# The plain tiles of a SwiGLU layer as a chunk of their own: chunks of 3, 7, 6 and 6 tiles in place of 4, 6, 6 and 6

## The chip, the cores and the metric

The kernel runs on one core of one Trainium2 chip. The core has a matrix engine (TensorE, PE in the profile, whose weight loads are PEld), a vector engine (VectorE, DVE), a scalar engine (ScalarE, ACT), a general engine (GpSimd, POOL) and SyncE (SP), which here only issues DMA transfers. Each engine works off its own instructions in order and waits for the others through semaphores. The metric is the device time of one execution in microseconds.

## The reference

A hybrid decoder trunk of two layers over 528 tokens (16 meta tokens and 512 others), with 1024 channels, in float32. Each layer has two half-step feed-forward blocks around a token mixer; every block is normalized ahead and behind:

```python
def swiglu(x, w_in, w_out):
    gate, up = jnp.split(x @ w_in, 2, axis=-1)
    return (jax.nn.silu(gate) * up) @ w_out

h = h + 0.5 * rmsnorm(swiglu(rmsnorm(h, g[0]), w_ffn_in[layer, 0], w_ffn_out[layer, 0]), g[1])
```

The gate and the up projection have 2816 columns each. That is 22 tiles of 128 hidden channels, each of which needs one block of gate and one of up weights (1024 x 128 each) and later one 128-row slice of `w_out`. There are four such feed-forward blocks, called l0f0, l0f1, l1f0 and l1f1 here; the tensor names of the profile leave out the last digit (`hidl1f` belongs to l1f0 and l1f1). The mixers between them, gated linear attention in layer 0 and windowed attention in layer 1, are not touched by the change. In the second layer the blocks run over the 512 tokens behind the meta tokens alone, in products of 256 or 512 columns; in the first over all 528, in products of 264, or of 272 and 256.

## The kernel before

**Three products for one.** Float32 precision is reached on the fast matmul type by splitting both operands into a high and a low part (`fp32r`). `mm3s` issues for each 128 x 128 block high times high, low times high and high times low. Every weight therefore passes through ACT (copy to the high part, L231 or L251) and DVE (subtraction to the low part, L232 or L252) before PE can use it.

**Weights.** `load_unit` issues the DMAs of a weight unit from SP into raw tiles of 128 x 512 (a pool of `RAWS` = 11), `split_unit` and `split_pair` split them into pair tiles of a second pool (`SLOTS` = 32). `set_ahead(n, slots)` says how far the loads may run ahead and how many slots the split weights may hold at once; a split that finds no slot waits until a product that used one has been issued (`slot`, `free_slots`).

**A feed-forward block** (`ffn`) takes its 22 tiles in the chunks of `FF_CHUNKS`. For each chunk the hidden tiles (named `hid...`) are made first, and then their part of the output projection (`out_proj`, `out_steps`; the products are named `y`) is added to the sum `Y` (named `Y`): the first chunk's part is written by ACT (L608), the later ones are added by DVE (L610).

- The first `PLAIN` = 3 tiles are made plainly: `x_first` makes the first two tiles (four units of 1024 x 128 weights) while the layer's input is still being normalized, and `x_units` makes the third tile. Their products are named `x`. Behind each stands a chain over DVE (L663, scale), ACT (L664, silu), DVE (L667, gate times up), ACT (L426, high part of hidden) and DVE (L427, low part).
- All other tiles are made by a Strassen scheme (class `Strassen`): gate and up are two rows, the two halves of the channels are the inner index, the two halves of the tokens are the columns, and seven block products replace eight. Each product is 4 x 3 = 12 matmuls. The products are called `11`, `s1`, `s2`, `12`, `s3`, `s4`, `22` after the weight part on the left; they go to PSUM tiles `a`, `c`, `d` (and `e` in a chunk's last tile). A zero matmul (`d<-zeros`) opens each chunk's tile `d`. The product `11` of the next tile stands ahead of `s4` and `22` of the tile at hand.
- The right sides of four of the products are sums of blocks of the layer's input. `right_factors` makes them once per block: eight scaled copies on ACT (L743, `xs...`), ten sums on DVE (L739), and eight splits (`z..._t`, four sums of two pieces: ACT L729 for the high part, DVE L730 for the low part). The weight sums `s1` to `s4` are made by accumulating DMAs from POOL (L257) and sums on DVE (L267, L272).

In the kernel before, the first chunk has three plain tiles and one Strassen tile, so its products that take a `z` stand right behind the third plain tile.

**Order.** The program is written by a small scheduler (`Flow`, `Job`), which runs in Python while the kernel is built: generators stand for chains of work, each `yield` gives an estimated delay, and the matmuls advance a modelled clock (`mm`). What a chain issues is placed in the program when the modelled clock reaches it. The order on every engine is thus fixed before the kernel runs. A waiting instruction holds up all those behind it on its engine.

In `out_steps`, when `jobs` are given, products of the first output rows with all hidden tiles but the last are placed ahead of the wait for the last one (`begin`).

Of the kernel before, what the change touches and what calls it, by code (L numbers as in the profile page):

```python
# [20 lines left out]
SEQ = 512  # L21
TOK = META + SEQ
NFF = 22
FF_CHUNKS = [(0, 4), (4, 10), (10, 16), (16, 22)]
LAST = 16
PLAIN = 3
NLAST = NFF - LAST
# [4 lines left out]
L1W = [(16, 512)]  # L32
SLOTS = 32
RAWS = 11
RING = 8
STEP = 1.1
LANDED = 2.2
ADDED = 2.5
# [90 lines left out]
def trunk_kernel(ctx: ExitStack, tc, a, out):  # L129
    nc = tc.nc  # L130
    pe, act, dve, pool, sp = nc.tensor, nc.scalar, nc.vector, nc.gpsimd, nc.sync
    flow = Flow()
# [19 lines left out]
    def pair_tile(name, dt=F32R):  # L152
        return hp.tile([P, 2, TOK], dt, tag="pair", name=name)

    def duo(name):
        t = pair_tile(name, F32)
        return t[:, 0], t[:, 1]
# [4 lines left out]
    def gain(layer, i, k):  # L162
        c = V_GAIN + layer * 48 + i * 8 + k
        return vec[:, c : c + 1]
# [19 lines left out]
    for layer in range(2):  # L184
        for f in range(2):
            for lo, hi in FF_CHUNKS:
                for t in range(lo, hi):
# [26 lines left out]
    def set_ahead(n, slots=None):  # L214
        ahead[0], limit[0] = n, slots or n
        room[0].finish(flow)
        room[0] = Job(None)
# [206 lines left out]
    def split(dst, src, g):  # L424
        o, n = g
        act.activation(dst[:, 0, o : o + n], src, AF.Copy)  # L426
        dve.tensor_tensor(dst[:, 1, o : o + n], src, dst[:, 0, o : o + n].bitcast(F32), op=ALU.subtract)  # L427
# [148 lines left out]
    def out_proj(*args, **named):  # L576
        for _ in out_steps(*args, **named):
            pass
# [71 lines left out]
    def ffn(x, groups, finish, opening=False, tail=4):  # L650
        set_ahead(8 if opening else 16)

        def evac_to(hids):
            gss = {}

            def evac(i, g, p):
                o, n = g
                r = x.rt[:, o : o + n]
                if i % 2 == 0:
                    if i not in gss:  # L660
                        gss[i] = duo("gu")
                    gs = gss[i][0][:, o : o + n]
                    dve.tensor_tensor(gs, p[:, :n], r, op=ALU.mult)  # L663
                    act.activation(gs, gs, AF.Silu)  # L664
                else:
                    gs, us = (t[:, o : o + n] for t in gss[i - 1])
                    dve.tensor_tensor(us, p[:, :n], gs, op=ALU.mult)  # L667
                    split(hids[i // 2], us, g)

            return evac  # L670

        jobs = []
        n2 = sum(n for _, n in groups) // 2
        halves = [(groups[0][0], n2), (groups[0][0] + n2, n2)]
        z = {}
        finish.x = x

        def new_hid():
            hids.append(pair_tile(f"hid{x.name}_{lo + len(hids)}"))
            return hids[-1]  # L680

        for ci, (lo, hi) in enumerate(FF_CHUNKS):
            hids = []
            if ci == 0:
                jobs = x_first(x, 4, evac_to([new_hid() for _ in range(2)]), opening)
                set_ahead(16, 4)
                flow.spawn(right_factors(x, halves, z))
                for t in range(2, PLAIN):
                    jobs += x_units(x, 2, groups, evac_to([new_hid()]))
                set_ahead(16, 8)  # L690
            else:
                set_ahead(16, RING)
            tiles = Strassen(x, z, halves)
            cur = tiles.head(new_hid())
            while cur:
                tiles.body(cur)
                nxt = tiles.head(new_hid()) if len(hids) < hi - lo else None
                if nxt is None:
                    fin = (finish, KD, True) if lo >= LAST else (None, 0, False)
                    if ci == 0:  # L700
                        flow.wait(*jobs)
                    proj = out_steps(hids, groups, x.groups, ci == 0, *fin, jobs)
                    end = used[0] + NLAST + tail
                jobs.append(tiles.tail(cur, proj if nxt is None else None))
                cur = nxt
            if lo >= LAST:
                set_ahead(32)
                cap[0] = min(end, len(units))
            for _ in proj:
                pass  # L710
# [538 lines left out]
    x = Operand("l0f0", lambda k: gain(0, 0, k), L0)  # L1249
# [48 lines left out]
    def into(name, layer, i, half, gv, groups, ffn=True):  # L1298
        nxt = Operand(name, gv, groups, ffn)
        return nxt, Residual(name, layer, i, half, nxt)  # L1300


    nxt, fin = into("l0m", 0, 1, True, lambda k: gain(0, 2, k), L0, False)
    ffn(x, L0, fin, True)
    x = nxt
    nxt, fin = into("l0f1", 0, 3, False, lambda k: gain(0, 4, k), L0)
    gla(x, fin)
    x = nxt
    nxt, fin = into("kv", 0, 5, True, lambda k: vec[:, V_KVN + k : V_KVN + k + 1], L0)
    ffn(x, L0, fin, tail=8)  # L1310


    with tc.tile_pool(name="kp", bufs=1) as kp:
        x = Operand("l1f0", lambda k: gain(1, 0, k), L1)
# [8 lines left out]
        nxt, fin = into("l1m", 1, 1, True, lambda k: gain(1, 2, k), L1, False)  # L1323
        ffn(x, L1W, fin)
        x = nxt
        nxt, fin = into("l1f1", 1, 3, False, lambda k: gain(1, 4, k), L1)
# [87 lines left out]
```

## Time and profile before

| | us |
|---|---|
| three runs | 1943.03, 1938.41, 1940.04 |
| median | 1940.04 |
| profiled execution, its own time | 1938.74 |
| span of the profiled execution, first to last instruction | 1937.0 |
| PE busy within the span | 1880.3 (97%) |
| DVE busy | 1377.9 (71%) |
| ACT busy | 1048.9 (54%) |
| POOL busy | 323.2 (17%) |
| mean granted clock of PE | 0.99 of full |

The profile is of one execution. A row of the timeline gives start, duration, engine, line, operation, out<-in and how many instructions are drawn together, then in brackets the idle time ahead of it and who ended it. Durations of neighbouring matmuls overlap (a matmul's end is modelled), so what a run of matmuls takes is read from start to start. A row of the windows view gives for one stretch its length, the busy time of PE, PEld, DVE, ACT and POOL with counts, the clock granted to PE (1.00 is full), and the DMA share and rate.

### The profile page before, as it was taken

To read this page: it belongs to the slowest core of one execution; us is meant where nothing else is said; L and a number is where in the kernel's file an instruction comes from. 1 tells how busy PE (TensorE), PEld (TensorE's weight loads), DVE (VectorE), ACT (ScalarE), POOL (GpSimd) and SP (SyncE) were. 2 spreads that over 40 slices of the span, in tenths; PEclk is the share of its full clock that TensorE was granted. 3 is DMA by queue.
4 is the path that set the end of the run, shared out by engine and by line. 5 is a ranking of instruction groups with operands and counts; after the bars stand their busy time and mean duration, and the time that the engine had idled before them with its cause. 6 is when DMAs were issued, how large, how long until landed. Compare 5 with 4: busy or idle time off the path is not lost.

```text
span 1937.0 us, 37708 instructions
## 1 busy us (share of the span) xinstructions
PE 1880.3 (97%) x14374; PEld 1789.6 (92%) x14374; DVE 1377.9 (71%) x2745; ACT 1048.9 (54%) x2349; POOL 323.2 (17%) x449
## 2 busy tenths in 40 slices
PE   8999999999999999999999999999988998999997
PEld 8999999999999999999999898989966897989897
DVE  7685858775464858585887685858798676858585
ACT  8563636663246755363675553636655675536363
POOL 2101010311212210101032101010342131010102
PEclk9999999999999999999999999999999998999998
DMA  6656565322113165656650556565320305565651
GB/s 200 152 141 154 141 153 157 97 80 74 38 62 110 49 153 137 153 143 152 161 150 24 142 139 160 143 160 164 101 77 23 88 23 143 140 159 143 166 144 44
DMA packets 134982, 234.44 MB, mean 121 GB/s; under 512 B 15120, under 2 KB 27920, under 8 KB 134800
## 3 DMA queue, kind: packets, MB, share of 16 engines
q1 hardware_dynamic: 112624, 192.04, 31.0%
q0 software_dynamic: 21888, 39.86, 13.6%
q8 instruction: 112, 1.84, 0.4%
q14 instruction: 70, 0.57, 0.1%
q10 hardware_dynamic: 288, 0.13, 0.0%
HBM read 229.87 MB, written 2.10 MB: 120 GB/s over the span
## 4 chain that ended last, share of the span: by engine, by line
PE 76%; DVE 13%; ACT 6%; issue 3%; DMA 1%; POOL 0%; SPq 0%; DVEq 0%; ACTq 0%; POOLq 0%
PE y L167 28%; PE a L167 18%; PE x L167 11%; PE c L167 8%; PE d L167 5%; DVE w L232 1%; PE e L167 1%; PE o L167 1%; ACT w L231 1%; DVE H L488 1%; DVE w L252 1%; DVE w_s L252 1%; PE po L167 1%; ACT w_s L251 1%; DMA raw<-in_w_last 0%
## 5 line engine op out<-in xcount | busy, mean ns | idle before, releaser
L252 DVE TENSOR_TENSOR w_s<-raw,w_s 128x512 fp32r<-128x512 f32 x304 | 207.8, 688 | 142.1 <-ACT w_s L251 140.7
L257 POOL DMA_DIRECT2D raw<-in_w_in x152 | 133.4, 929 | 1032.3 <-DMA raw<-in_w_in 363.0
L167 PE MATMUL y<-hidl0f,w 128*128 128x256 f32 (+1 forms) x2112 | 261.4, 285 | 0.0
L232 DVE TENSOR_TENSOR w<-raw,w 128x512 fp32r<-128x512 f32 x362 | 234.4, 667 | 35.9 <-ACT w L231 33.1
L167 PEld LDWEIGHTS y<-hidl0f,w 128*128 128x128 f32 x2112 | 259.1, 188 | 0.2
L251 ACT ACTIVATE w_s<-raw 128x512 fp32r<-128x512 f32 x304 | 184.7, 626 | 130.0 <-DVE raw L267 75.9
L167 PE MATMUL y<-hidl1f,w 128*128 128x512 f32 (+1 forms) x1344 | 250.2, 346 | 0.0
L167 PEld LDWEIGHTS y<-hidl1f,w 128*128 128x128 f32 x1344 | 211.9, 188 | 32.4
L231 ACT ACTIVATE w<-raw 128x512 fp32r<-128x512 f32 x362 | 198.8, 584 | 54.4 <-PE y L167 44.9
L252 DVE TENSOR_TENSOR w<-raw,w 128x512 fp32r<-128x512 f32 x228 | 153.4, 687 | 41.0 <-ACT w L251 38.4
L251 ACT ACTIVATE w<-raw 128x512 fp32r<-128x512 f32 x228 | 137.4, 620 | 43.7 <-PE y L167 42.6
L167 PE MATMUL x<-x_l0m,w 128*128 128x272 f32 (+1 forms) x1200 | 157.6, 288 | 0.0
L167 PEld LDWEIGHTS x<-x_l0m,w 128*128 128x128 f32 x1200 | 149.2, 189 | 1.1
L610 DVE TENSOR_TENSOR Y<-y,Y 128x256 f32<-128x256 f32 (+2 forms) x176 | 82.2, 472 | 68.6 <-PE y L167 68.2
L167 PE MATMUL a<-zl0f_t,w_s 128*128 128x264 f32 x912 | 125.1, 286 | 3.0 <-ACT w_s L251 1.7
L167 PE MATMUL a<-zl1f_t,w_s 128*128 128x256 f32 x912 | 121.5, 282 | 0.1
L167 PEld LDWEIGHTS a<-zl0f_t,w_s 128*128 128x128 f32 x912 | 116.5, 188 | 4.7 <-ACT w_s L251 1.9
L167 PEld LDWEIGHTS a<-zl1f_t,w_s 128*128 128x128 f32 x912 | 113.1, 188 | 2.0 <-ACT c L797 1.5
L422 POOL TENSOR_TENSOR acc_post<-acc_post,sq_post 128x256 f32<-128x256 f32 (+1 forms) x72 | 62.2, 864 | 252.4 <-ACT sq_post L421 251.3
L814 ACT ACTIVATE c<-c 128x264 f32<-128x264 f32 (+1 forms) x76 | 32.0, 421 | 131.4 <-DVE c L813 131.4
L167 PE MATMUL x<-x_l0f,w 128*128 128x272 f32 (+1 forms) x576 | 75.5, 292 | 6.7 <-ACT w L231 5.7
L167 PEld LDWEIGHTS x<-x_l0f,w 128*128 128x128 f32 x576 | 73.5, 193 | 7.8 <-ACT w L231 5.7
(368 smaller groups left out, 3533.4 us busy)
## 6 DMA issues: line engine op xcount, KB each, us to landing
raw<-in_w_in SPq DMA_DIRECT2D x428, 256.0 KB, 3.6
raw<-in_w_in POOLq DMA_DIRECT2D x152, 256.0 KB, 5.1
raw<-in_w_out SPq DMA_DIRECT2D x96, 256.0 KB, 3.4
raw<-in_gla_in SPq DMA_DIRECT2D x50, 256.0 KB, 3.3
raw<-in_w_last SPq DMA_DIRECT2D x48, 256.0 KB, 2.9
raw<-in_w_out SPq DMA_DIRECT2D x64, 128.0 KB, 2.9
raw<-in_gla_out SPq DMA_DIRECT2D x16, 256.0 KB, 2.7
raw<-in_w_q SPq DMA_DIRECT2D x16, 256.0 KB, 4.2
```

The costliest lines, as they stand in the source:

```text
L167: inst = pe.matmul(o, lhs, rhs, start=start, stop=stop, skip_group_check=onto)
L231: act.activation(w[:, 0, :m], raw[:, :m], AF.Copy)
L232: dve.tensor_tensor(w[:, 1, :m], raw[:, :m], w[:, 0, :m].bitcast(F32), op=ALU.subtract)
L251: act.activation(w[:, 0, :512], src, AF.Copy)
L252: dve.tensor_tensor(w[:, 1, :512], src, w[:, 0, :512].bitcast(F32), op=ALU.subtract)
L257: pool.dma_start(dst, src, accum_op=ALU.add)
L422: pool.tensor_tensor(sums[0][:, :n], sums[0][:, :n], t[:, :n], op=ALU.add)
L488: dve.tensor_tensor(h, t, h, op=ALU.add)
L610: dve.tensor_tensor(y, p[:, :n], y, op=ALU.add)
L814: act.activation(t.u2, t.u2, AF.Silu)
```

## The change

`FF_CHUNKS` becomes 3, 7, 6 and 6 tiles. The first chunk now holds the three plain tiles alone. When their hidden tiles are issued, the output projection of these three follows at once, and the loop goes on to the next chunk; no product is placed ahead of the wait for the third hidden tile by `begin`, since no `jobs` are given to `out_steps` there. The job that makes the sums of operand blocks (`right_factors`) is kept in `factors`, and the second chunk's first Strassen tile is issued after it. Seven tiles are in the second chunk, of which each is made as before.

The slot limit follows: 4 slots while the sums are being made (as before), 8 once they are issued (`widen`), and in the Strassen chunks `RING` less the chunk's tiles: 14 - 7 = 7 slots in the second chunk, 14 - 6 = 8 in the third and fourth, where it was 8 in all.

The units of `w_out` change their width: a unit of the first chunk has 8 row blocks of 3 x 128 = 384 columns (before 512), a unit of the second 7 x 128 = 896 columns, loaded as 512 and 384 (before 512 and 256).

```diff
-FF_CHUNKS = [(0, 4), (4, 10), (10, 16), (16, 22)]
+FF_CHUNKS = [(0, 3), (3, 10), (10, 16), (16, 22)]
...
-RING = 8
+RING = 14
...
                 jobs = x_first(x, 4, evac_to([new_hid() for _ in range(2)]), opening)
                 set_ahead(16, 4)
-                flow.spawn(right_factors(x, halves, z))
+                factors = flow.spawn(right_factors(x, halves, z))
+
+                def widen():
+                    yield factors
+                    set_ahead(16, 8)
+
+                flow.spawn(widen())
                 for t in range(2, PLAIN):
                     jobs += x_units(x, 2, groups, evac_to([new_hid()]))
-                set_ahead(16, 8)
-            else:
-                set_ahead(16, RING)
+                flow.wait(*jobs)
+                out_proj(hids, groups, x.groups, True)
+                continue
+            flow.wait(factors)
+            set_ahead(16, RING - (hi - lo))
             tiles = Strassen(x, z, halves)
...
-                    if ci == 0:
-                        flow.wait(*jobs)
-                    proj = out_steps(hids, groups, x.groups, ci == 0, *fin, jobs)
+                    proj = out_steps(hids, groups, x.groups, False, *fin, jobs)
```

Lines below the edit stand six further down in the changed kernel: L729, L730, L739 and L743 are L735, L736, L745 and L749 there.

The instructions of all engines are the same in number and kind, but for the widths told above and four zero matmuls less (one for each first chunk). Their order differs only in the first two chunks of each of the four blocks.

TensorE in l1f1, behind the last `x` product of the third plain tile. In the kernel before, the order is this (`w_11`, `w_s` and `w_12` are weight parts, `zl1f_t` a sum of operand blocks; what a row waits for stands in brackets):

```order
L167 MATMUL x_0_19459<-x_l1f_7_19109,w_1_19337 128x512 x3
L167 MATMUL d_19505<-zeros 128x256
L167 MATMUL a_0_19501<-x_l1f_0_18931,w_11_19469 128x256 [waits PE_49,Activation_49]
L167 MATMUL a_0_19501<-x_l1f_0_18931,w_11_19469 128x256 [waits DVE_49]
...
L167 MATMUL c_0_19503<-zl1f_t_19537,w_s_19486 128x256 [waits PE_49,Activation_49]
L167 MATMUL c_0_19503<-zl1f_t_19537,w_s_19486 128x256 [waits DVE_49]
L167 MATMUL d_19505<-x_l1f_4_19034,w_12_19540 128x256 [waits Activation_49]
```

In the changed kernel the same place has the output projection of the three plain tiles (`y_0_16` and `y_1_16` are the first and second output rows, `hidl1f_0` to `hidl1f_2` the three hidden tiles):

```order
L167 MATMUL x_0_19439<-x_l1f_7_19085,w_1_19321 128x512 x3
L167 MATMUL y_0_16_19481<-hidl1f_0_19025,w_0_19324 128x512 [waits Activation_49]
L167 MATMUL y_0_16_19481<-hidl1f_0_19025,w_0_19324 128x512 [waits DVE_49] x2
L167 MATMUL y_0_16_19481<-hidl1f_1_19026,w_0_19324 128x512 [waits Activation_49]
L167 MATMUL y_0_16_19481<-hidl1f_1_19026,w_0_19324 128x512
L167 MATMUL y_0_16_19481<-hidl1f_1_19026,w_0_19324 128x512 [waits DVE_49]
L167 MATMUL y_1_16_19494<-hidl1f_0_19025,w_0_19327 128x512 [waits PE_49]
L167 MATMUL y_1_16_19494<-hidl1f_0_19025,w_0_19327 128x512
L167 MATMUL y_0_16_19481<-hidl1f_2_19386,w_0_19324 128x512 [waits Activation_49]
```

The products with `zl1f_t` have moved behind the 72 matmuls of the output projection, and the third hidden tile is now asked for by the ninth matmul behind the last `x` product.

VectorE at the same place, between the low parts of the second and the third hidden tile. Before:

```order
L427 TENSOR_TENSOR hidl1f_1_19050<-gu,hidl1f_1_19050 128x256 [waits Activation_49]
L252 TENSOR_TENSOR w_11_19469<-raw_0_19382,w_11_19469 128x512 [waits DMAHW6_49,Activation_49]
L739 TENSOR_TENSOR xsl1f_0_19407<-xsl1f_4_19409,xsl1f_0_19407 128x2x256 [waits Activation_49]
L739 TENSOR_TENSOR xsl1f_4_19409<-xsl1f_4_19409,xsl1f_0_19407 128x2x256 [waits DVE_49]
L252 TENSOR_TENSOR w_s_19486<-raw_3_19385,w_s_19486 128x512 [waits DMASW2_49,Activation_49]
L667 TENSOR_TENSOR gu<-x_0_19459,gu 128x512 [waits PE_49]
L739 TENSOR_TENSOR xsl1f_2_19408<-xsl1f_6_19410,xsl1f_2_19408 128x2x256 [waits Activation_49]
L739 TENSOR_TENSOR xsl1f_4_19409<-xsl1f_4_19409 128x2x256 [waits DVE_49]
L427 TENSOR_TENSOR hidl1f_2_19402<-gu,hidl1f_2_19402 128x512 [waits Activation_49]
```

In the changed kernel:

```order
L427 TENSOR_TENSOR hidl1f_1_19026<-gu,hidl1f_1_19026 128x256 [waits Activation_49]
L745 TENSOR_TENSOR xsl1f_0_19391<-xsl1f_4_19393,xsl1f_0_19391 128x2x256 [waits Activation_49]
L667 TENSOR_TENSOR gu<-x_0_19439,gu 128x512 [waits PE_49]
L745 TENSOR_TENSOR xsl1f_2_19392<-xsl1f_6_19394,xsl1f_2_19392 128x2x256 [waits Activation_49]
L745 TENSOR_TENSOR xsl1f_4_19393<-xsl1f_4_19393,xsl1f_0_19391 128x2x256 [waits DVE_49]
L427 TENSOR_TENSOR hidl1f_2_19386<-gu,hidl1f_2_19386 128x512 [waits Activation_49]
L232 TENSOR_TENSOR w_0_19498<-raw_0_19378,w_0_19498 128x384 [waits DMAHW2_49,Activation_49]
```

The two splits of the first Strassen tile's weights and one of the sums have moved behind the third hidden tile's last instruction.

ScalarE in l1f1, ahead of the second half of the plain tiles' evacuation. Before, two splits of a plain unit stand there (L231), followed by three scaled copies (L743). In the changed kernel four splits of `w_out` units have come in between:

```order
L231 ACTIVATE w_1_19321<-raw_512_19203 128x512 [waits DMAHW5_49]
L231 ACTIVATE w_0_19324<-raw_0_19205 128x384 [waits DMAHW6_49]
L231 ACTIVATE w_0_19327<-raw_0_19207 128x384 [waits DMAHW7_49]
L231 ACTIVATE w_0_19342<-raw_0_19209 128x384 [waits DMAHW0_49]
L231 ACTIVATE w_0_19345<-raw_0_19211 128x384 [waits DMAHW1_49]
L749 ACTIVATE xsl1f_0_19391<-H,vec 128x512 x2
L399 ACT_TABLE_LOAD
L399 ACTIVATE R_l1f_19102<-st_l1f_272_19372,eps 128x256 [waits PE_49]
```

One scaled copy that stood ahead of the table load now stands behind it, and the four splits stand ahead of it.

## The prediction, made before the changed kernel was run

> **What bounds the kernel now.** I read the page first, then the chain of work that ended last, then PE's waits, and last the four places that the change touches.
>
> ```profile
> span 1937.0 us, 37708 instructions
> PE 1880.3 (97%) x14374; PEld 1789.6 (92%) x14374; DVE 1377.9 (71%) x2745; ACT 1048.9 (54%) x2349; POOL 323.2 (17%) x449
> PE 76%; DVE 13%; ACT 6%; issue 3%; DMA 1%; POOL 0%; SPq 0%; DVEq 0%; ACTq 0%; POOLq 0%
> ```
>
> PE is busy for 97% of the span, and three quarters of the chain are its own. The amount of PE's work hardly changes here, so the change can only win what PE idles, or works at a lower clock. What PE waited for, longest first (total, times, longest one); these four rows fall into the first chunks:
>
> ```profile
> PE c L167 <- ACT zl1f_t L729: 11.1, 2, 6.4
> ...
> PE d L167 <- ACT w L251: 1.8, 1, 1.8
> PE a L167 <- ACT w_s L251: 1.7, 1, 1.7
> ...
> PE c L167 <- ACT zl0f_t L729: 1.6, 1, 1.6
> ```
>
> The largest wait in the program is for the sums of operand blocks (`zl1f_t`) in layer 1. The timeline of PE at its worst place, l1f1, shows how it stands:
>
> ```profile
> 1596.86 0.28 PE L167 MATMUL d<-zeros 128*128 128x256 f32 x1
> 1597.85 0.38 PE L167 MATMUL a<-x_l1f,w 128*128 128x256 f32 x1 [0.72 <-ACT w L251]
> 1598.58 1.55 PE L167 MATMUL a<-x_l1f,w 128*128 128x256 f32 x11 [0.34 <-DVE w L252]
> 1606.51 0.80 PE L167 MATMUL c<-zl1f_t,w_s 128*128 128x256 f32 x2 [6.38 <-ACT zl1f_t L729]
> ...
> 1610.16 2.27 PE L167 MATMUL d<-x_l1f,w 128*128 128x256 f32 x11
> 1612.26 1.11 PE L167 MATMUL e<-x_l1f,w_s 128*128 128x256 f32 x8
> ```
>
> The plain tiles' products end at 1596.86. Three Strassen products (`a`, `c`, `d`) then take until 1612.26. Eleven matmuls of `d` needed 2.10 us there (1610.16 to 1612.26), much more than elsewhere, so idle time is not all. The windows view from the last plain product to the end of the third Strassen product, for l0f0, l0f1, l1f0, l1f1 (length, then busy time of PE, PEld, DVE, ACT and POOL with counts; the third number from the end is the granted clock):
>
> ```profile
> 47.00:54.40 7.40, 4.95 (x39) 4.54 (x38) 7.16 (x14) 6.67 (x14) 0.00 (x0) 1.00 0.31 94
> 672.40:683.40 11.00, 6.75 (x38) 5.82 (x37) 10.07 (x18) 6.93 (x15) 0.94 (x2) 0.85 0.42 131
> 1068.20:1079.70 11.50, 6.74 (x38) 6.52 (x37) 9.63 (x16) 7.10 (x14) 0.88 (x1) 0.70 0.35 81
> 1597.00:1612.20 15.20, 7.51 (x38) 6.66 (x37) 13.42 (x23) 10.27 (x20) 0.87 (x1) 0.66 0.38 97
> sum 45.10, PE 25.95 PEld 23.53 DVE 40.28 ACT 30.97 POOL 2.70; mean PE 6.49 PEld 5.88 DVE 10.07 ACT 7.74 POOL 0.67
> ```
>
> So 45.10 us for 12 products. DVE is nearly full there (40.28 of 45.10): it makes the sums, and PE waits for it through ACT. In three of the four the clock fell too (0.85, 0.70, 0.66). What undisturbed work takes is read from start to start:
>
> ```profile
> 122.31 1.63 PE L167 MATMUL a<-x_l0f,w 128*128 128x264 f32 x12
> ...
> 125.23 1.64 PE L167 MATMUL a<-zl0f_t,w 128*128 128x264 f32 x12
> ...
> 132.55 1.61 PE L167 MATMUL a<-x_l0f,w 128*128 128x264 f32 x12
> 147.81 33.42 PE L167 MATMUL y<-hidl0f,w 128*128 128x256 f32 x273
> 181.07 0.29 PE L167 MATMUL d<-zeros 128*128 128x264 f32 x1
> 1703.97 30.19 PE L167 MATMUL y<-hidl1f,w 128*128 128x512 f32 x129
> 1733.99 0.28 PE L167 MATMUL d<-zeros 128*128 128x256 f32 x1
> 1734.11 1.57 PE L167 MATMUL a<-x_l1f,w 128*128 128x256 f32 x12
> ```
>
> Seven products between 122.31 and 132.55: 1.463 us each at 264 columns, by proportion 1.42 at 256. A `y` matmul takes 33.26 / 273 = 0.122 us in layer 0 and 30.02 / 129 = 0.233 us (512 columns) in layer 1. Twelve products should take 6 x 1.463 + 6 x 1.42 = 17.3 us. The loss is 45.1 - 17.3 = **27.8 us**: 3.0, 6.6, 7.2 and 10.9 in the four blocks.
>
> **The change, part by part.**
>
> *The Strassen tile leaves the first chunk.* It moves to the second chunk with its 84 matmuls, its evacuation, its weights and its part of the output projection; none of it is saved. Gone is the wait: -27.8, if the sums are done when the second chunk begins, and if the place is not taken by another wait.
>
> *Four zero matmuls less.* 1733.99 to 1734.11 is 0.12 us; four are -0.5.
>
> *The sums beside the output projection.* PE now has 72 `y` matmuls of 0.233 us, 16.8 us, in each block of layer 1, and 144 of 0.122, 17.6 us, in layer 0. In that time DVE has 20 instructions to issue between the third hidden tile and the second chunk (eight splits of `z`, three sums, four splits of `w_out`, four of weight parts, one sum of weight parts); at 0.6 us each, as the DVE rows below follow each other, that is 12 us. In l1f1 it starts at about 1602 and PE ends its `y` at 1597.3 + 1.6 + 16.8 = 1615.7 (worked out below), so 1.7 us are left. The last sums are not needed at the first product either but up to seven products later. Cost 0; if that cover is gone, a `z` comes late again in the second chunk (a rival).
>
> *What is late next: the third hidden tile.* Before, the Strassen products stood between the third plain tile and the output projection. Now the ninth matmul behind the last plain product asks for it. In l1f1 its chain was (ACT rows, then DVE rows):
>
> ```profile
> 1586.22 0.42 ACT L426 ACTIVATE hidl1f<-gu 128x256 fp32r<-128x256 f32 x1 [1.01 <-DVE gu L667]
> 1586.55 1.14 ACT L231 ACTIVATE w<-raw 128x512 fp32r<-128x512 f32 x2
> 1587.59 1.94 ACT L743 ACTIVATE xsl1f<-H,vec 128x512 f32<-128x512 f32 x3
> ...
> 1601.10 0.63 ACT L426 ACTIVATE hidl1f<-gu 128x512 fp32r<-128x512 f32 x1 [0.94 <-DVE gu L667]
> ```
>
> ```profile
> 1596.40 0.76 DVE L427 TENSOR_TENSOR hidl1f<-gu,hidl1f 128x256 fp32r<-128x256 f32 x2 [0.38 <-ACT hidl1f L426]
> ...
> 1600.39 0.68 DVE L667 TENSOR_TENSOR gu<-x,gu 128x512 f32<-128x512 f32 x1
> ...
> 1602.19 0.68 DVE L427 TENSOR_TENSOR hidl1f<-gu,hidl1f 128x512 fp32r<-128x512 f32 x1
> ```
>
> Two things shift it. Four `w_out` splits of 384 columns now stand ahead of ACT's table load: between 0.33 us (256 columns, 1586.22 to 1586.55) and 0.52 (512 columns, 1586.55 to 1587.59 for two), so about 0.42 each, 1.7 in all; one scaled copy of 0.65 went behind. The queue is 1.0 us later, and so are the first two hidden tiles: PE waits some 0.5 us at its first `y`. Against that, DVE has two weight splits and a sum less between L427 and L667, 1.9 us. Step by step: ACT ends the second hidden tile at about 1597.65, two copies at 1598.95, DVE the sum at 1599.6 and L667 at 1600.2, ACT the high part at 1600.85. PE, started at 1597.3, has run its eight matmuls by 1599.2 and waits 1.6. In l1f1 that is **+2.1** (bounds 0.5, the first wait alone, and 4.0: nothing won on DVE, so that the high part comes 1.0 behind its 1601.73 of before, 3.5 behind 1599.2).
>
> In l0f1 the rows are these:
>
> ```profile
> 673.99 0.43 ACT L426 ACTIVATE hidl0f<-gu 128x272 fp32r<-128x272 f32 x1 [1.91 <-DVE gu L667]
> ```
>
> ```profile
> 673.51 0.77 DVE L667 TENSOR_TENSOR gu<-x,gu 128x272 f32<-128x272 f32 x2
> ```
>
> The plain products end at 672.3, nine `y` matmuls at 0.122 cover 1.1 us, until 673.4. The high part was there at 674.4. The queue's shift (+1.0 to +1.7) and two weight splits fewer on DVE (-1.2) leave it between 674.1 and 676.0: a wait of 0.7 to 2.6. I take **+1.4**, nearer the lower end, since DVE and not ACT released L426 here. In l0f0 and l1f0 L667 waited for PE itself, so the queues have room and the splits of `w_out` fit into it:
>
> ```profile
> 46.83 0.77 DVE L667 TENSOR_TENSOR gu<-x,gu 128x272 f32<-128x272 f32 x2 [0.31 <-PE x L167]
> ```
>
> ```profile
> 1068.30 0.69 DVE L667 TENSOR_TENSOR gu<-x,gu 128x512 f32<-128x512 f32 x1 [0.27 <-PE x L167]
> ```
>
> The high part then comes about 1.3 us behind the last plain product, and eight or nine `y` matmuls cover 1.1 to 1.9. I take **+0.1** each (0 to 1.4, the latter what l0f1 is given).
>
> *The clock.* The rows above show it at 1.00 in l0f0, with 7.40 us that held 3.0 of loss, and at 0.85 in l0f1, where 0.15 x 11.0 = 1.65 us were lost to it. A wait as I expect it in l0f1 or l1f1 lies between these; I charge one such drop, **+1.65** (bounds 0 and four of them, 6.6). [...]
>
> *Seven slots instead of eight in the second chunk.* The slot goes to the seventh hidden tile. DVE's split of the next tile's part `11` is the last of the two in this row:
>
> ```profile
> 129.89 1.29 DVE L252 TENSOR_TENSOR w<-raw,w 128x512 fp32r<-128x512 f32 x2
> ```
>
> It starts at 130.5 and is used at 132.55. With seven slots it needs the slot of product `22` of the tile before, issued at 125.23 and done by 126.7, with nearly 4 us to spare (ACT's half needs some 0.6 of them). Cost 0 (bounds 0 and one product per tile, the rival below).
>
> *Narrower `w_out` units.* DMAs to landing:
>
> ```profile
> raw<-in_w_out SPq DMA_DIRECT2D x96, 256.0 KB, 3.4
> ...
> raw<-in_w_out SPq DMA_DIRECT2D x64, 128.0 KB, 2.9
> ```
>
> 192 KB lie between. They are issued in the order of use, no wait of PE's above names a DMA, and their number is the same: 0.
>
> The sum: -27.8 - 0.5 + 0.1 + 0.1 + 1.4 + 2.1 + 1.65 = -22.95. The profiled execution took 1938.74 us (span 1937.0), so the changed kernel would take 1915.8 by it. The median shown is 1.3 above the profiled one; I forecast for the median **1917 us**, a gain of 23.
>
> **The rivals.**
>
> *The third hidden tile becomes the new stall.* ACT and DVE are in-order queues, and the sums stand among the instructions that make it. If all four blocks wait 2.1 us and drop the clock once each, that is 4 x (2.1 + 1.65) = 15.0 in place of 5.35: 1917 + 9.65 = 1927. For it speaks that DVE is nearly full in these stretches; against it, that two of the blocks have room in the queues, and that fewer instructions stand ahead of it than before.
>
> *Seven slots choke the second chunk (slower).* If every part came one product later and none of it were covered, each of the tiles would lose a product: 7 x (2 x 1.463 + 2 x 1.42) = 40 us, 1957. It decides from 23 / 28 = 0.82 us per tile of the second chunk. The lead of part `11` is only 1.4 us (131.2 to 132.55), which speaks for it; the slot that is free 4 us ahead speaks against.
>
> *The sums are late all the same.* If DVE gets behind during the output projection, the second chunk starts with the old wait. With some 2 us to spare and 12 us to do, a fifth more of DVE time would use that up; 2 us per block would give 1917 + 8 = 1925.
>
> **How the numbers follow.** Forecast 0.68, hidden tile 0.17, slots 0.08, sums late 0.07. A difference under 0.2% (3.9 us) can't be told from no change here. Faster by more: the forecast, the hidden tile and half of the last case, whose price can grow past 2 us per block: 0.88. Slower: the slots, 0.08. Within: the other half of the last case, 0.04. The forecast's own range is 1911 to 1924: all new waits at their lower ends and no drop gives -27.8 - 0.5 + 1.2 = -27.1, 1913, less 2 for the spread of the runs; the upper bounds of the two waits and two more drops give some 7 more. With the second and the fourth case the range is 1909 to 1931.
>
> **What would show it.** Right: no row of PE waiting for `zl1f_t` or `zl0f_t` above 1 us; PE going from `x` to `y` at 47, 672, 1068 and 1597 (less the gain so far), with short waits there for L426 and L427; a granted clock near 1.00 in these stretches but for one; the second chunk's products at 1.42 to 1.46 us from start to start. Wrong: waits of PE for L251 or L252 at the parts of the second chunk (slots), or a wait for `z` at its start (sums late), or waits for `hidl0f` and `hidl1f` of over 3 us (hidden tile).

## The result and the profile after

| | before | changed |
|---|---|---|
| runs, us | 1943.03, 1938.41, 1940.04, 1941.07 | 1920.44, 1918.89, 1919.28, 1919.39 |
| median, us | 1940.55 | 1919.34 |
| profiled execution, us | 1938.74 | 1920.44 |
| its span, us | 1937.0 | 1918.7 |

The ratio is 0.9891, with a 95% interval of 0.9874 to 0.9908: 21.2 us less at the medians, where 23 were forecast. The head of the page and the chain of the changed kernel:

```profile
span 1918.7 us, 37680 instructions
PE 1877.7 (98%) x14370; PEld 1786.4 (93%) x14370; DVE 1379.7 (72%) x2741; ACT 1045.8 (55%) x2349; POOL 322.9 (17%) x449
PE 72%; DVE 15%; ACT 6%; DMA 4%; issue 3%; POOL 0%; SPq 0%; DVEq 0%; ACTq 0%; POOLq 0%
```

But for four zero matmuls on PE and four additions on VectorE (2741 instructions for 2745), all engines do the same work as before. The additions are those that each chunk's last Strassen tile needs for its product in `e`; the account of the change above names the zero matmuls alone. PE's waits (total, times, longest):

```profile
PE y L167 <- ACT hidl1f L426: 1.8, 2, 1.4
...
PE y L167 <- ACT hidl0f L426: 1.5, 1, 1.5
...
PE a L167 <- ACT c L803: 0.8, 2, 0.5
```

The rows for `zl1f_t` and `zl0f_t` are gone; the waits for the third hidden tile have come. Where they lie, on PE's timeline in l0f1 and in l1f1:

```profile
668.83 1.27 PE L167 MATMUL y<-hidl0f,w 128*128 128x272 f32 x9
671.65 16.65 PE L167 MATMUL y<-hidl0f,w 128*128 128x272 f32 x135 [1.55 <-ACT hidl0f L426]
688.14 0.29 PE L167 MATMUL d<-zeros 128*128 128x264 f32 x1
688.26 1.62 PE L167 MATMUL a<-x_l0f,w 128*128 128x264 f32 x12
689.72 1.64 PE L167 MATMUL c<-zl0f_t,w_s 128*128 128x264 f32 x12
```

```profile
1587.48 2.12 PE L167 MATMUL y<-hidl1f,w 128*128 128x512 f32 x8 [0.40 <-ACT hidl1f L426]
1591.00 15.08 PE L167 MATMUL y<-hidl1f,w 128*128 128x512 f32 x64 [1.40 <-ACT hidl1f L426]
1605.91 0.28 PE L167 MATMUL d<-zeros 128*128 128x256 f32 x1
1606.03 1.58 PE L167 MATMUL a<-x_l1f,w 128*128 128x256 f32 x12
1607.44 1.59 PE L167 MATMUL c<-zl1f_t,w_s 128*128 128x256 f32 x12
```

The products of the second chunk follow each other at 1.41 to 1.46 us with no idle time before a `z`. The windows view of the four output projections of plain tiles (length, busy PE, PEld, DVE, ACT, POOL; the third number from the end is the granted clock):

```profile
47.04:64.61 17.57, 17.57 (x147) 17.57 (x146) 14.52 (x25) 14.90 (x36) 3.48 (x4) 1.00 0.65 177
668.83:688.14 19.31, 17.76 (x146) 17.55 (x145) 16.58 (x28) 15.08 (x36) 2.57 (x3) 1.00 0.49 121
1059.73:1076.53 16.80, 16.80 (x74) 13.37 (x73) 13.64 (x23) 13.93 (x27) 2.60 (x3) 1.00 0.53 132
1587.08:1605.91 18.83, 17.03 (x72) 13.40 (x73) 17.39 (x31) 16.44 (x33) 2.75 (x4) 1.00 0.59 137
```

The clock is at 1.00 in all four. DVE and ACT are now nearly full in the output projection (17.39 and 16.44 of 18.83 us in l1f1), where PE is too.

To see what each block won, I take the time from the end of its plain products to the begin of its third chunk. Both kernels do the same work between these marks: seven Strassen tiles and the output projection of ten tiles. The marks are read from PE's timelines; the forecast column repeats the terms of the prediction by block (loss, less new waits, plus a zero matmul).

| | before, us | changed, us | won | forecast |
|---|---|---|---|---|
| l0f0 | 134.1 | 130.3 | 3.8 | 3.0 |
| l0f1 | 137.2 | 132.1 | 5.1 | 5.3 |
| l1f0 | 133.3 | 126.6 | 6.7 | 7.3 |
| l1f1 | 137.1 | 128.5 | 8.6 | 9.0 |
| sum | 541.7 | 517.6 | 24.1 | 24.6, less 1.65 for a clock drop |

These marks repeat well: a second profile of the changed kernel gives 517.7. The spans, however, differ by 18.3 only. Of the other 5.8, 5.0 were lost where nothing was changed: from l1f0's fourth chunk to the end of l1f1's plain products, mostly the attention mixer of layer 1, the profile of before took 301.9 us and that of after 306.9. The windows view of 100 us of that mixer, of before and of the changed kernel:

```profile
1415.01:1515.01 100.00, 88.53 (x608) 61.29 (x607) 85.84 (x241) 54.70 (x228) 26.75 (x26) 0.97 0.15 46
```

```profile
1400.18:1500.18 100.00, 88.48 (x586) 60.68 (x584) 83.01 (x232) 52.98 (x221) 26.78 (x26) 0.91 0.14 46
```

PE has the same order of work there and was busy as long, but 22 matmuls less got done at a clock of 0.91 in place of 0.97. By these rounded figures 9 of the 100 us went to the lower clock there in place of 3, which is the size of the whole difference. How far this is chance is taken up with the repeated runs below.

### The profile page after: what moved, and what is told of

Same layout as the page of the kernel before. It is cut to its first block, busy times and chain, and to the rows that moved or that the text cites. A ratio compares the mean times of both kernels' runs of the same rounds, so it can differ in the third digit from the quotient of the medians.

```text
span 1918.7 us, 37680 instructions
## 1 busy us (share of the span) xinstructions
PE 1877.7 (98%) x14370; PEld 1786.4 (93%) x14370; DVE 1379.7 (72%) x2741; ACT 1045.8 (55%) x2349; POOL 322.9 (17%) x449
## 4 chain that ended last, share of the span: by engine, by line
PE 72%; DVE 15%; ACT 6%; DMA 4%; issue 3%; POOL 0%; SPq 0%; DVEq 0%; ACTq 0%; POOLq 0%
PE y L167 29%; PE a L167 16%; PE x L167 11%; PE c L167 7%; PE d L167 4%; DMA raw<-in_w_in 2%; DVE w L252 1%; DVE w L232 1%; PE o L167 1%; PE e L167 1%; DVE H L488 1%; DVE w_s L252 1%; ACT w L231 1%; DMA raw<-in_w_last 1%; PE po L167 1%
## 5 line engine op out<-in xcount | busy, mean ns | idle before, releaser
L232 DVE TENSOR_TENSOR w<-raw,w 128x512 fp32r<-128x512 f32 (+1 forms) x362 | 233.6, 668 | 42.2 <-ACT w L231 39.7
L231 ACT ACTIVATE w<-raw 128x512 fp32r<-128x512 f32 (+1 forms) x362 | 198.5, 585 | 72.9 <-PE y L167 56.0
L252 DVE TENSOR_TENSOR w<-raw,w 128x512 fp32r<-128x512 f32 x228 | 153.0, 688 | 31.9 <-ACT w L251 28.6
L251 ACT ACTIVATE w<-raw 128x512 fp32r<-128x512 f32 x228 | 136.9, 620 | 36.7 <-PE y L167 36.6
L167 PEld LDWEIGHTS a<-zl1f_t,w_s 128*128 128x128 f32 x912 | 112.8, 188 | 2.8 <-ACT c L803 2.2
```

What stands on the lines that cost most here:

```text
L167: inst = pe.matmul(o, lhs, rhs, start=start, stop=stop, skip_group_check=onto)
L231: act.activation(w[:, 0, :m], raw[:, :m], AF.Copy)
L232: dve.tensor_tensor(w[:, 1, :m], raw[:, :m], w[:, 0, :m].bitcast(F32), op=ALU.subtract)
L251: act.activation(w[:, 0, :512], src, AF.Copy)
L252: dve.tensor_tensor(w[:, 1, :512], src, w[:, 0, :512].bitcast(F32), op=ALU.subtract)
```

## The experiments

The theory: PE's loss in the first chunk was a wait for what ACT and DVE had not got done, with the lower clock that came with it, and the output projection of the plain tiles is cover enough for it. The rivals: it was the sums alone that were late; the cover isn't needed; a slot less costs; the waits for the third hidden tile can be taken away. "The four stretches" below are the sums of the table above. The kernel before had medians of 1940.55 to 1945.35 on the chips used, so each ratio is to before on the same chip.

### Were the sums what PE waited for?

In the kernel before, the first chunk's Strassen tile takes plain blocks of the input in place of the sums:

```diff
+            zc = z
+            if ci == 0:
+                same = {"t1": "11", "t2": "21", "t3": "22", "t4": "11"}
...
-            tiles = Strassen(x, z, halves)
+            tiles = Strassen(x, zc, halves)
```

> The kernel before, but the first chunk's one Strassen tile multiplies by plain blocks of the layer's input where it took the four sums (t1 by 11, t2 by 21, t3 by 22, t4 by 11); this part of the computation is changed. The sums are still made, for the later chunks. If the sums are what PE waits for, at least half of the 27.8 us goes: 1922 us (1917 to 1930), no row of PE waiting for zl0f_t or zl1f_t, what is left being waits for weight parts. If the weight parts, which stand in the same queues of ACT and DVE, are as late as the sums, little goes: 1933 to 1941, with rows of PE waiting for w and w_s of L251 and L252 in place of those for the sums.

Measured: 1938.95 us (1937.50 to 1943.57), ratio 0.998 (0.9966 to 0.9993). The four stretches took 537.4 us, 4.3 less than before; most of the loss stayed. PE's waits, and its timeline in l1f1:

```profile
PE a L167 <- ACT w_s L251: 11.7, 4, 3.9
```

```profile
1601.47 1.56 PE L167 MATMUL c<-x_l1f,w_s 128*128 128x256 f32 x11 [0.26 <-DVE w_s L252]
1606.95 0.58 PE L167 MATMUL a<-x_l1f,w_s 128*128 128x256 f32 x1 [3.92 <-ACT w_s L251]
1608.22 2.72 PE L167 MATMUL a<-x_l1f,w_s 128*128 128x256 f32 x11 [0.69 <-DVE w_s L252]
```

The second product (`c`) runs now, and the third (`a`, weight part `s2`) waits in its place. The sums were only what came last; the weight parts were nearly as late.

Next the sums are left out of the whole kernel, so that they take no time of ACT and DVE either:

```diff
     def right_factors(x, halves, z):
...
-        xs = [pair_tile(f"xs{x.name}_{k}", F32) for k in range(0, KD, 2)]
...
-        yield from part("t4", b21)
+        for t, b in (("t1", "11"), ("t2", "21"), ("t3", "22"), ("t4", "11")):
+            z[t] = z[b]
+            ready[t].finish(flow)
+        yield 0
```

> The kernel before, with the sums of operand blocks left out altogether: all Strassen tiles multiply by plain blocks of the layer's input instead, so that this part of the computation is missing. If the queues of ACT and DVE as a whole set the end of the wait (18 DVE instructions of 0.6 us are gone, 11 us a block), weight parts come in time too: at most 1.5 us of waits are left per block in the first chunk and the time is 1940 - 24 = 1916 (1912 to 1920). If the weight parts are late by themselves (the accumulating DMA from POOL, the four slots, the planner's delays): the waits for w_s of the run without waits for sums stay at 2 to 4 us a block, 1925 to 1938.

Measured: 1927.58 us (1927.47 to 1930.74), ratio 0.9926 (0.9903 to 0.9949). The four stretches took 526.3 us, 15.4 less than before and still 8.7 more than the changed kernel, which makes all the sums. Neither expectation holds as a whole: waits for `s2` are left, 1.5 us in each block of layer 0 and 2.7 in each of layer 1. PE's row for it, and DVE in l1f1 around it:

```profile
PE a L167 <- ACT w_s L251: 7.1, 4, 2.4
```

```profile
1595.04 0.69 DVE L667 TENSOR_TENSOR gu<-x,gu 128x512 f32<-128x512 f32 x1 [0.82 <-PE x L167]
1596.43 0.69 DVE L427 TENSOR_TENSOR hidl1f<-gu,hidl1f 128x512 fp32r<-128x512 f32 x1 [0.70 <-ACT hidl1f L426]
...
1597.64 0.69 DVE L252 TENSOR_TENSOR w_s<-raw,w_s 128x512 fp32r<-128x512 f32 x1
...
1598.90 0.69 DVE L267 TENSOR_TENSOR raw<-raw,raw 128x512 f32<-128x512 f32 x1
1600.28 0.69 DVE L252 TENSOR_TENSOR w_s<-raw,w_s 128x512 fp32r<-128x512 f32 x1 [0.69 <-ACT w_s L251]
```

The splits of `s3` and `s2` stand behind the third hidden tile in the queue of DVE, and that tile waits for PE's last plain product (0.82). From there to `s2` it is 5.9 us (1595.04 to 1600.97), and PE has only two products, 2.8 us, to run. So the waits of before had two sources: the time that DVE needs for the sums, and an order in which the first Strassen tile's parts stand behind the third plain tile. Which of the planner's delays and slot limits puts the parts there was not tested. Moving the Strassen tile behind the output projection takes both out of PE's way.

Part of what this run won is the clock. The windows view from the end of the plain products, in l1f0 and l1f1 (in layer 0 the clock was at 1.00 there):

```profile
1063.15:1076.00 12.85, 10.11 (x71) 9.71 (x70) 9.68 (x17) 8.13 (x17) 1.75 (x2) 0.87 0.46 118
1594.84:1608.20 13.36, 10.67 (x74) 10.27 (x73) 10.09 (x18) 8.54 (x18) 1.74 (x2) 0.87 0.59 161
```

That is 0.13 of 12.85 and of 13.36 us, 3.4 us lost to the clock. The four rows of the prediction give 0.15 of 11.0, 0.30 of 11.5 and 0.34 of 15.2 us for the kernel before, 10.3 us. So of the 15.4 us won without the sums some 6.9 are clock and 8.5 are waits.

### Is the output projection the cover?

First the sums were begun only when the output projection had been written:

```diff
-                factors = flow.spawn(right_factors(x, halves, z))
...
                 flow.wait(*jobs)
                 out_proj(hids, groups, x.groups, True)
+                factors = flow.spawn(right_factors(x, halves, z))
...
                 continue
```

> The changed kernel, but the sums are begun only when the output projection of the three plain tiles has been issued. If the output projection is the cover that makes the change pay, each block now waits for the sums at the start of the second chunk: eight copies and the first two sums and splits make 6 to 8 us ahead of the first product with a sum, the next sums some 2 to 4 more, and the clock falls: 10 to 12 us a block, 1919 + 44 = 1963 (1945 to 1980). If the sums would be hidden anyway, by the Strassen tile's products with plain blocks and the splits: 1919 to 1925.

Measured: 1919.33 us (1917.97 and 1920.69), against 1963 expected. The miss lies in the edit. ScalarE's timeline in l1f1 shows the copies (L749) between the evacuations (L608), from the third one on:

```profile
1594.81 0.60 ACT L608 ACTIVATE Y<-y 128x512 f32<-128x512 f32 x1 [0.65 <-PE y L167]
1595.64 0.63 ACT L251 ACTIVATE w_s<-raw 128x512 fp32r<-128x512 f32 x1 [0.23 <-DVE raw L267]
1596.18 1.32 ACT L749 ACTIVATE xsl1f<-H,vec 128x512 f32<-128x512 f32 x2
1597.41 0.58 ACT L608 ACTIVATE Y<-y 128x512 f32<-128x512 f32 x1
```

What is written later in the program may still stand earlier in an engine's queue when it depends on nothing that is late. The sums thus lay beside the second half of the output projection, and that was nearly enough: the four stretches took 520.2 us, 2.6 more than in the changed kernel.

So the first copy was tied behind the last evacuation (`after`, which the program has for an order within ScalarE):

```diff
+                last_y[0] = act.activation(y, p[:, :n], AF.Copy)
...
-            act.activation(xs[k // 2][:, k % 2, : 2 * n], H[:, k, o : o + 2 * n], AF.Identity, scale=x.gv(k))
+            after(last_y[0], act.activation(xs[k // 2][:, k % 2, : 2 * n], H[:, k, o : o + 2 * n], AF.Identity, scale=x.gv(k)))
```

> The changed kernel, but the first copy of the sums is tied behind ScalarE's last evacuation of the plain tiles' output projection, so that none of the sums lies beside it. If the cover is what the change lives on: eight copies on ACT (5 us), ten sums and eight splits on DVE (11 us) now stand ahead of the second chunk's products, PE waits some 6 to 8 us for the first sum and as much again in pieces for the others, and the clock falls: 8 to 14 us a block, 1919 + 44 = 1963 (1951 to 1975). If the Strassen tile's own products and splits would hide them: under 1930.

Measured: 1955.56 us (1954.51 to 1958.15), ratio 1.0063 (1.0039 to 1.0087): slower than before. The four stretches took 556.8 us, 39 more than in the changed kernel, 9.8 a block. PE's waits:

```profile
PE c L167 <- ACT zl1f_t L737: 9.2, 2, 4.6
PE c L167 <- ACT zl0f_t L737: 8.9, 2, 4.4
...
PE d L167 <- ACT w L251: 5.2, 4, 1.9
```

The granted clock fell as well: 0.80, 0.79, 0.79 and 0.73 over 17.4, 16.0, 16.0 and 19.1 us from the end of the output projection, some 15 of the 39 us. So the cover, the clock that it keeps up included, is worth more than the whole gain. A chunk of three plain tiles alone, with the sums behind it in this order, is a loss.

### Can the waits for the third hidden tile go?

Three edits aimed at the 3.35 us that are left. The sums begun behind the third hidden tile:

```diff
                 flow.wait(*jobs)
+                factors = flow.spawn(right_factors(x, halves, z))
...
                 out_proj(hids, groups, x.groups, True)
```

> The changed kernel, but the sums are begun when the third hidden tile has been issued, just ahead of the output projection. If the sums' place ahead of the third hidden tile in ACT's and DVE's queues makes the remaining waits of 1.55 and 1.80 us, both go, and the second chunk keeps its rate if 16.8 us of cover are enough: 1919.3 - 3.3 = 1916. If the cover is too short from there, waits for zl0f_t, zl1f_t or w at the second chunk's begin take the place, as much as is won: 1919 to 1921.

Measured: 1920.51 us (1920.39 to 1921.89), ratio 0.9884 (0.9865 to 0.9904). The waits for hidden tiles are gone, and in their place:

```profile
PE a L167 <- ACT w L251: 3.7, 4, 1.1
```

That is a wait for the weight parts of the second chunk's second tile, whose splits now stand behind the last `z`. The four stretches took 521.2 us, 3.6 more. What is begun later ends later, though DVE is not full here. DVE in l1f1, and the windows view of the output projection there:

```profile
1604.11 3.94 DVE L736 SCALAR_TENSOR_TENSOR zl1f_t<-xsl1f,zl1f_t 128x512 fp32r<-128x512 f32 x6
1587.25:1604.04 16.79, 16.79 (x73) 13.36 (x72) 12.86 (x21) 14.77 (x28) 2.30 (x3) 1.00 0.57 141
```

DVE was busy for 12.86 of 16.79 us, as it waited again and again for ACT, whose copies stand between the evacuations, and six of the eight low parts of the `z` come only behind the output projection.

The `w_out` splits put behind ACT's table load, by 12 slots instead of 16 while the first two plain tiles are made:

```diff
-                jobs = x_first(x, 4, evac_to([new_hid() for _ in range(2)]), opening)
+                jobs = x_first(x, 4, evac_to([new_hid() for _ in range(2)]), opening, first_ahead=6)
```

> The changed kernel, with 12 slots instead of 16 while the first two plain tiles are made, so that no split of a w_out unit stands ahead of ACT's table load. If these four splits shift the hidden tiles by 1.0 us: in l1f1 the first wait of 0.40 goes and that of 1.40 falls to 0.4, in l0f1 1.55 falls to 0.5. If the splits only move to another place ahead of the first output products: waits for w of L231 or L232 of the same size in their place.

Measured: one run of 1914.42 us. PE waits 1.0 us in l0f1 (1.55 in the changed kernel) and, in l1f1, nothing at the first output product but 1.65 at the third hidden tile (0.40 and 1.40): two of the splits have moved between the second hidden tile and the copies. The first expectation (0.5 and 0.4 left) fell short. The four stretches took 517.1 us, 0.5 less. This run is 6.0 us under the profiled run of the changed kernel (1920.44); its mixer of layer 1 took 302.1 us, which explains 4.8 of them.

More output products ahead of the wait:

```diff
-                flow.wait(*jobs)
-                out_proj(hids, groups, x.groups, True)
+                out_proj(hids, groups, x.groups, True, jobs=jobs)
```

> The changed kernel, with the output projection's first two (512 columns) or three (272 and 256) output rows run with the first two hidden tiles ahead of the wait for the third: 18 matmuls instead of 9 in layer 0, 12 instead of 8 in layer 1. If PE waits there for the third hidden tile alone, 1.1 of the 1.55 us go in l0f1 and 0.9 of the 1.40 in l1f1: 1919.3 - 2.0 = 1917.3. If something else is late at the same time (the low part, the w_out splits), the wait only changes its name: 1919.3 within 1.

Measured: 1918.35 us (1917.07 to 1920.96), ratio 0.9872 (0.9850 to 0.9895). The high part's wait fell to 0.46 us in both blocks, and the low part's came up. PE in l1f1:

```profile
1588.32 0.74 PE L167 MATMUL y<-hidl1f,w 128*128 128x512 f32 x2 [0.46 <-ACT hidl1f L426]
1589.49 13.68 PE L167 MATMUL y<-hidl1f,w 128*128 128x512 f32 x58 [0.43 <-DVE hidl1f L427]
```

The four stretches took 517.4 us, 0.2 less: the first expectation (2.0) fell.

To tell such small differences apart, three kernels ran side by side, the changed one among them, and one with both of the last two edits:

> The changed kernel once more, unchanged, for the spread of its runs beside the next two on one chip. In its first profile the mixer of layer 1 (from the fourth chunk of l1f0 to the end of the plain products of l1f1) took 306.9 us at a lower clock in four places, before 301.9 at fewer. If that is chance of the clock: a profile may show 302 to 307, and the runs lie between 1914 and 1920. If the changed kernel brings it about: 306 to 307 again and no run under 1918.

> The kernel with the w_out splits behind ACT's table load, once more with rounds. Its one run took 1914.42, with 302.1 us in the mixer of layer 1. If the w_out splits are worth what its waits show (2.6 us of waits for hidden tiles in place of 3.3, and none at the first output product): 1.0 to 1.5 under the changed kernel on the same chip. If the one run was good by the mixer's clock alone: the same within 0.5.

> Both edits together, w_out splits behind the table load and more output products ahead of the wait for the third hidden tile. If they add up (the one is worth 1.0 to 1.5, the other 1.0 as measured): 2.0 to 2.5 under the changed kernel on the same chip, waits for hidl0f and hidl1f under 1.5 in all. If the low part of the third hidden tile then sets the end: no better than either alone.

| | median, us | runs | ratio to before | four stretches | l1f0's 4th chunk to l1f1's plain end |
|---|---|---|---|---|---|
| changed, again | 1918.97 | 1918.45 to 1920.75 | 0.9880 (0.9865 to 0.9895) | 517.7 | 303.6 |
| splits later | 1917.23 | 1915.34 to 1919.24 | 0.9869 (0.9855 to 0.9884) | 517.0 | 305.5 |
| both edits | 1916.16 | 1914.09 to 1918.79 | 0.9862 (0.9845 to 0.9880) | 516.8 | 305.4 |

Both edits have the lowest median of several runs, but their interval overlaps that of the changed kernel, and the stretches that the edits touch show 0.9 of the 2.8 us. PE's waits for hidden tiles are 1.3 us in all there (0.93 and 0.41, in l1f1), as expected, but less of that is won. Whether it beats the changed kernel stays open. The last column shows what hides it: the mixer's time differs by 5 us between profiles of kernels that have the same order of work there, and by 3 between two profiles of the same kernel (306.9 and 303.6, the splits-later kernel 302.1 and 305.5).

Of the two expectations for the changed kernel's repeat, each holds by half: its mixer took 303.6 us, not 306 to 307 again, but no run lay under 1918. So part of the spread is chance, since one and the same kernel showed 306.9 and 303.6. Whether the changed order makes a fall of the clock in the mixer more likely stays open: the three profiles of the kernel before that still make the sums took 301.9, 302.0 and 302.7 us there, the ten of the changed kernel and its variants 302.1 to 306.9, and the one without sums 307.3.

### Does a slot less cost anything?

The kernel before with `RING = 7`, and the changed one with `RING = 13` (6 slots in the second chunk, 7 in the third and fourth):

> The kernel before with 7 slots in the second to fourth chunk in place of 8. If a slot less costs nothing, as the 4 us that a slot is free ahead of part 11 say: 1940.5 within 2. If 7 slots choke the chunk, up to one product of 1.42 to 1.46 us for each of 18 tiles in four blocks: up to 104 us, and anything above 1944 speaks for it.

> The changed kernel with one slot less again: 6 slots in the second chunk, 7 in the third and fourth. The second chunk took 112.8 us in layer 0 and 109.8 in layer 1 with 7 slots. If a slot is free nearly 4 us ahead with 7 slots, it still is 2.3 us ahead with 6 (a product less): 112.8 and 109.8 within 0.5, 1919 within 2. If 7 slots were just enough: a wait of PE for weight parts in each of the seven tiles, 0.3 us or more a tile, 115 and 112 or more, above 1927.

Measured: 1940.17 us (1939.31 to 1944.80), ratio 0.9987 (0.9973 to 1.0000); and 1917.72 us (1914.76 to 1918.57), ratio 0.9873 (0.9855 to 0.9890). Second chunks of the first: 96.5, 96.6, 93.7 and 93.7 us, where the profile of before has 96.9, 96.8, 93.8 and 93.8. Of the second: 112.7, 112.7, 109.8 and 109.9 with 6 slots, 112.8, 112.8, 109.8 and 109.7 with 7. A slot less costs nothing, nor do two.

The run with `RING = 7` showed something else. In l0f0 its first chunk has the same waits as the profile of before, 1.68 and 0.77 us, but not the same clock:

```profile
51.95 0.39 PE L167 MATMUL a<-zl0f_t,w_s 128*128 128x264 f32 x1 [1.68 <-ACT w_s L251]
53.11 2.79 PE L167 MATMUL a<-zl0f_t,w_s 128*128 128x264 f32 x11 [0.77 <-DVE w_s L252]
55.70 2.84 PE L167 MATMUL d<-x_l0f,w 128*128 128x264 f32 x12
58.34 2.02 PE L167 MATMUL a<-zl0f_t,w_s 128*128 128x264 f32 x12
60.19 1.64 PE L167 MATMUL e<-x_l0f,w_s 128*128 128x264 f32 x12
```

The same place in the profile of before:

```profile
53.02 1.61 PE L167 MATMUL a<-zl0f_t,w_s 128*128 128x264 f32 x11 [0.77 <-DVE w_s L252]
...
57.73 1.61 PE L167 MATMUL e<-x_l0f,w_s 128*128 128x264 f32 x12
```

From 53.11 to 60.19 it is 7.08 us; there the same matmuls took 4.71. The windows view of the run with `RING = 7`, ahead of the fall and behind it:

```profile
48.90:52.30 3.40, 1.72 (x13) 1.35 (x11) 3.40 (x7) 3.21 (x7) 0.00 (x0) 1.00 0.24 77
52.40:59.20 6.80, 6.09 (x27) 6.09 (x28) 4.74 (x10) 3.47 (x9) 1.72 (x2) 0.50 0.56 139
```

The clock fell at about 52.4, behind the first wait and when the second had hardly begun. Up to this place the two kernels issue the same instructions in the same order, so behind the same waits the clock fell in one execution and not in the other, at 2.4 us here.

## Why the prediction came out as it did

**The loss of 27.8 us.** It held in size. The stretches won 24.1; with the new waits of 3.35 and without the zero matmuls (0.5) that is 24.1 + 3.35 - 0.5 = 27.0. By the clock column of the prediction's own four rows 10.3 of the 27.8 were lost to the lower clock and 17.5 to waits; with the waits gone, both came back. Reading it as the difference between elapsed and undisturbed time of the whole stretch, and not from the row of one wait, made it safe against what that row got wrong: the prediction said that DVE makes the sums and PE waits for it, and the runs without sums showed that the weight parts and their place behind the third plain tile made up a good part of it. That part of the mechanism was incomplete, and the forecast was safe from it because the change moves the weight parts as well.

**The third hidden tile.** It held, by place and size: +0.1, +1.4, +0.1 and +2.1 were forecast, 0, 1.55, 0 and 1.80 measured. In l1f1 the two waits were worked out as 0.5 and 1.6 and came as 0.40 and 1.40. The 1.0 us laid to the four `w_out` splits is shown only in part: with the splits later, the waits fell by 0.5 in l0f1 and by 0.15 in l1f1, where two of them came to stand ahead of the copies.

**The clock.** This is the step that failed: +1.65 for one drop, and the clock stayed at 1.00 in all four stretches. On what was won there the forecast was so some 1.1 us too low (22.95 against 24.1). A drop was not unfounded: in the kernel before with `RING = 7` the clock did fall behind a wait of 1.68 us, and in l0f1 of the kernel before, where no single wait is over 1.82 us, it was at 0.85. The waits of about 1.55 and 1.40 us left it at 1.00, in the second profile of the changed kernel and in that with six slots too.

**Sums beside the output projection, slots, narrower units: 0.** They held. No row waits for a `z`; 7 slots, and even 6, cost nothing; no wait for a DMA came up there. That the Strassen tile's own time is only moved shows in the second chunk: 112.8 us in l0f0, where six tiles took 96.9; a tile is seven products (10.24) and 48 `y` (5.86), 16.1, and 96.9 + 16.1 = 113.0.

**The median.** 1917 was forecast, 1919.34 measured, though the blocks won a little more than forecast. What was not thought of is the mixer of layer 1, whose clock (0.97 and 0.91 over 100 us of it) and time (302 to 307 us) differ between executions and were taken as equal. The profiled execution of before had the good end of it. For the two profiled executions this term is measured (5.0 us); that it also moved the medians is likely, but not shown, as the other runs have no trace. One profile can't show such a term, but the spread of the runs hints at it: 1938.41 to 1943.03. So that the median came within 3 us of the forecast is partly luck: 1.1 us too little in the stretches, and the mixer the other way.

**The rivals.** The slots are shown to be free. The hidden tile took its expected price and no more. The sums were never late in the changed kernel; the forced order, in which they are, cost 39 us.

## What to carry to other kernels

Price a stall by elapsed less undisturbed time of its whole stretch: the row of a wait names only what came last, and with that taken away the next in the same queue takes its place (11.7 us of waits for `w_s` here). Where a stage feeds itself through in-order engines, put work between it and its consumer that needs none of what is late, and check that the engines behind have as much time there as they need: here 12 us of DVE work fitted into 17 us of matmuls, and with DVE and ACT then nearly full (17.39 and 16.44 of 18.83 us in l1f1), the further shifts tried won at most 0.9 us there or moved the wait. Look at the clock of the stretch beside its waits: here more than a third of what a stall cost, 10.3 of 27.8 us, was the clock that fell with it. What is written later in a program isn't thereby issued later; read it from the timeline.

## What the runs showed of the hardware

The same two waits of 1.68 and 0.77 us, in the same order of instructions, left the clock at 1.00 in one execution; in another it was at 0.50 from about 52.4 to 59.2 us, and the matmuls there took 2.4 us longer. What decided between the two was not shown. In the second, PE had been busy for 1.72 of the 3.40 us ahead of the fall. The waits of about 1.55 and 1.40 us in the changed kernel and its six-slot variant left the clock at 1.00 in three profiles. In this kernel's attention mixer, where PE waits twelve times in 100 us, 11.4 us in all, two profiles show a clock of 0.97 and 0.91 over these 100 us from the same place. The mixer's time differs by 3 to 5 us between executions (301.9 and 306.9, 306.9 and 303.6), as much as a small change is worth.
